# A transformer block on one core: the opening of its first feed-forward layer taken one token tile at a time

## The chip, the cores and the metric

The kernel runs on one core of a Trainium2 chip. The metric is device time in microseconds (us) of one launch, the median of three runs. The core has five engines that run in parallel, each with its own in-order list of instructions: TensorE (PE in the profile; its weight loads are PEld), VectorE (DVE), ScalarE (ACT), GpSimd (POOL) and SyncE (SP), which here only issues transfers. SBUF is the on-chip memory; PSUM holds what PE accumulates.

## The reference, cut to what matters

One block: a feed-forward layer (FFN), a mixer of attention and convolution, a second FFN. Each is preceded by an RMS norm whose result is modulated by a shift and a scale, and followed by a gate. Shifts, scales and gates are 9 x 2048 numbers, one product of a vector with a matrix of 2048 x 18432 (151 MB). There are 256 tokens, D = 2048, F = 5632, all in fp32.

```
ada = einsum('bd,de->be', silu(c), w_ada) + b_ada
sh1, sc1, g1, shm, scm, gm, sh2, sc2, g2 = split(ada, 9)
h = modulate(rms_norm(x, ffn1_norm), sh1, sc1)      # h * (1 + sc) + sh
x = x + 0.5 * g1 * swiglu(h, ffn1_w_gu, ffn1_w_down)
```

## The kernel before

**Tiles.** The 256 tokens are two token tiles of 128 (t = 0, 1). The depth of 2048 is 16 slices of 128, which this document calls k-rows; four of them are one piece (kb or pc, 0 to 3). The 2 x 5632 columns of the first product are 22 chunks of 512 columns (256 of the gate, 256 of the other half). A "row" of work is one k-row of one chunk for both token tiles. Every operand is split into a high and a low part, and a product is three matmuls (`mm3`, lines 315 to 317): high x high, high x weight's low, low x weight's high. A row is thus six matmuls of 128x512. A weight comes as fp32 from memory; ACT casts its high part (lines 294, 308), DVE subtracts to get the low part (lines 296, 309).

**The ada lines.** `w_ada` is stored as 144 lines of 1 MB, each 128 outputs x 2048. `ada(j)` (line 175) loads line j into one of four buffers (`rawp`, shared with the 1 MB weight tiles) and reduces it on DVE against `c_bc`, the activated c spread over all partitions. A k-row of the normed input needs two lines, its scale and its shift; for the first FFN, k-row k needs lines 2k and 2k+1. `ada_due` (line 195) spreads the loads: `DUE` is a table of (rows of work, lines to have asked for by then), read by straight lines between its points.

**The opening of the first FFN** (`ffn`, line 441, branch `if not st.done`, lines 479 to 516). The order is written out:
- At line 116 to 118 the small constants and both token tiles of x are loaded. Lines 746 to 748 sum the squares of both tiles. `begin_both` (line 390) normalizes the first 512 columns of both tiles and transposes them into two PSUM buffers.
- `first_modulation` (line 228) loads lines 0 and 1 in halves, with chunk 0's first weight row between them, and reduces each half.
- `begin_ready` modulates a k-row for both tiles as soon as its two lines have been asked for: `Norm.tile` (line 380), one ACT and two DVE operations.
- Chunks 0 to 7 first run with one k-row, 8 to 11 with two, 12 to 14 with three, the others with all four of the first piece (`EXT`). `LOADS` says which chunks share a transfer; work on a load follows its transfer by `AHEAD` = 3 loads. `FIRST_ADA` gives the ada lines asked for after each of the first twelve loads; after that `DUE` does. The result of a chunk goes from PSUM to a part in SBUF by an ACT copy (line 468).

**After the opening.** The chunks of `AGAIN` (4, 5, 6) get the rest of their first piece in PSUM, which `add_part` (line 535, DVE) adds to the part. `EARLY` lists groups of chunks that then run their rest with pieces 1 and 2. The second normed piece is made when ada lines up to 16 have been asked for (`pieces`). All else comes later and is not touched.

**What sets the order.** The program's text gives the order in which work is offered; a list scheduler places an instruction on its engine as soon as its estimated time comes, so that a later one that is ready can go ahead of an earlier one that is not. `tc.issue_after(ins)` keeps what it encloses behind `ins` on the same engine's list. Buffers come from pools: 28 blocks of 4 KB a partition (`blkp`), four each of high and low weight buffers of two rows (`whp`, `wlp`), six PSUM accumulators, two PSUM buffers for transposes.

## Time and profile before

| | |
|---|---|
| Median of 3 runs | 1859.41 us (1859.16 to 1860.31) |
| The profiled execution | 1858.73 us |
| Its span | 1857.0 us, granted TensorE clock 0.994 |
| PE busy | 1823.5 us, 98% |
| DVE busy | 1442.8 us, 78% |
| ACT busy | 910.7 us, 49% |
| Transfers | 495.91 MB, 267 GB/s on average |

The span runs from the first to the last instruction of the program; the execution's own time is 1.7 us longer. "Busy" counts an engine's own instructions, not waits. A row of the timeline is: start, duration, engine and line, operation, what it writes and from what, and in brackets how long the engine had been idle and what ended that. A row of the waits is: who waited for whom, total us, times, longest. "PEclk" is the clock granted to TensorE, 1.00 being full. SPq is SP issuing a transfer; the transfer's data comes later.

### The profile page before, as it was taken

Reading aid. Unit: us, or ns where it says so; the run is one execution under the profiler, and the core shown is the slowest. Engines: PE = TensorE matmul, PEld = TensorE weight load, DVE = VectorE, ACT = ScalarE, POOL = GpSimd, SP = SyncE. Lnnn points to the kernel's source line nnn. Section 1 sums busy time; section 2 is a strip of 40 time slices with the busy share of each in tenths; the row PEclk is TensorE's granted clock in tenths of the full one; section 3 lists DMA queues with packets and bytes.
Section 4 is the critical chain, followed back from the end, with each engine's and each line's share of the span. In section 5 each row is a group of like instructions: output and inputs, shape, how many; then the busy total and the mean of one; then the engine's idle time right before and its main releaser. Section 6 shows DMA issues by size and latency. Waiting matters only on the chain.

```text
span 1857.0 us, 21888 instructions
## 1 busy us (share of the span) xinstructions
PE 1823.5 (98%) x8247; PEld 1503.3 (81%) x8247; DVE 1442.8 (78%) x1922; ACT 910.7 (49%) x1378; POOL 28.8 (2%) x29
## 2 busy tenths in 40 slices
PE   6999999999999999999999899999999999999999
PEld 5788888888888887888888688888888888888887
DVE  7788869998888778789899968878877755544553
ACT  6553444444444443554776545664444444433332
POOL 0000000000000000000110000000000000000000
PEclk8999999999999999999999899999999999999999
DMA  9888968889989898645444667888777755556552
GB/s 384 336 318 302 344 253 317 336 297 342 328 327 367 341 355 331 241 178 181 159 159 159 249 227 276 338 321 333 269 279 281 281 182 194 191 206 213 196 212 79
DMA packets 72730, 495.91 MB, mean 267 GB/s; under 512 B 8193, under 2 KB 8625, under 8 KB 15153
## 3 DMA queue, kind: packets, MB, share of 16 engines
q1 hardware_dynamic: 72624, 494.53, 71.6%
q8 instruction: 64, 1.05, 0.2%
q14 instruction: 42, 0.34, 0.0%
HBM read 492.37 MB, written 2.12 MB: 266 GB/s over the span
## 4 chain that ended last, share of the span: by engine, by line
PE 91%; DVE 4%; DMA 2%; ACT 1%; issue 1%; POOL 0%; SPq 0%; POOLq 0%; DVEq 0%; ACTq 0%
PE acc L316 30%; PE acc L317 30%; PE acc L315 29%; DMA blk<-in_w_gu_dram 1%; DVE wlo L296 1%; DVE blk L771 1%; PE tp L588 1%; DMA raw<-in_w_ada_dram 1%; PE acc L863 1%; PE tp L377 1%; ACT whi L294 0%; DVE raw L181 0%; ACT tmp L825 0%; POOL rv L978 0%; DVE blk L923 0%
## 5 line engine op out<-in xcount | busy, mean ns | idle before, releaser
L294 ACT CAST whi<-raw 128x1024 fp32r<-128x1024 f32 (+1 forms) x605 | 628.0, 1046 | 751.7 <-PE acc L317 605.8
L296 DVE TENSOR_TENSOR wlo<-raw,whi 128x1024 fp32r<-128x1024 f32 (+1 forms) x605 | 724.7, 1211 | 319.8 <-ACT whi L294 318.7
L315 PE MATMUL acc<-whi,blk 128*128 128x512 f32 x2448 | 957.4, 393 | 10.8 <-ACT blk L990 4.8
L316 PE MATMUL acc<-wlo,blk 128*128 128x512 f32 x2448 | 956.9, 391 | 2.5 <-DVE wlo L296 2.5
L317 PE MATMUL acc<-whi,blk 128*128 128x512 f32 x2448 | 956.1, 391 | 1.1 <-DVE blk L991 1.1
L315 PEld LDWEIGHTS acc<-whi,blk 128*128 128x128 f32 x2448 | 460.9, 188 | 107.3 <-ACT blk L990 5.1
L316 PEld LDWEIGHTS acc<-wlo,blk 128*128 128x128 f32 x2448 | 461.3, 188 | 99.3 <-DVE wlo L296 5.6
L317 PEld LDWEIGHTS acc<-whi,blk 128*128 128x128 f32 x2448 | 460.5, 188 | 98.8 <-DVE blk L991 1.8
L181 DVE CUSTOM_DVE_ANT_0 raw<-raw,c_bc 128x2048 f32<-128x2048 f32 x142 | 324.2, 2284 | 10.1 <-DMA raw<-in_w_ada_dram 9.9
L771 DVE SCALAR_TENSOR_TENSOR blk<-blk,cst,blk 128x255 f32<-128x255 f32 (+14 forms) x240 | 97.6, 458 | 0.0
L468 ACT COPY blk<-acc 128x512 f32<-128x512 f32 x88 | 49.8, 591 | 60.3 <-PE acc L317 58.4
L580 DVE TENSOR_TENSOR blk<-acc,blk 128x512 f32<-128x512 f32 x88 | 56.7, 682 | 0.1
L315 PE MATMUL acc<-blk,blk 128*128 128x512 f32 x112 | 43.9, 393 | 0.0
L317 PE MATMUL acc<-blk,blk 128*128 128x512 f32 x112 | 43.8, 391 | 0.0
L316 PE MATMUL acc<-blk,blk 128*128 128x512 f32 x112 | 43.6, 389 | 0.0
L296 DVE TENSOR_TENSOR blk<-raw,blk 128x1024 fp32r<-128x1024 f32 x28 | 33.8, 1220 | 2.1 <-ACT blk L294 1.9
L582 DVE TENSOR_TENSOR blk<-blk 128x256 f32<-128x256 f32 x88 | 33.3, 417 | 0.5 <-ACT blk L581 0.5
L581 ACT ACTIVATE blk<-blk 128x256 f32<-128x256 f32 x88 | 32.2, 411 | 1.4 <-DVE blk L580 1.4
L294 ACT CAST blk<-raw 128x1024 fp32r<-128x1024 f32 x28 | 28.9, 1050 | 7.7 <-DMA raw<-in_w_dn_dram 6.5
L334 DVE TENSOR_TENSOR blk<-tp,blk 128x512 fp32r<-128x512 f32 x44 | 29.9, 684 | 1.8 <-ACT blk L333 1.8
L343 ACT ACTIVATE tmp<-xall 128x512 f32<-128x512 f32 x22 | 13.8, 632 | 30.1 <-DVE xall L641 16.7
L333 ACT CAST blk<-tp 128x512 fp32r<-128x512 f32 x44 | 25.3, 580 | 2.4 <-PE tp L588 2.4
(149 smaller groups left out, 665.9 us busy)
## 6 DMA issues: line engine op xcount, KB each, us to landing
raw<-in_w_gu_dram SPq DMA_DIRECT2D x161, 1024.0 KB, 5.3
raw<-in_w_ada_dram SPq DMA_DIRECT2D x142, 1024.0 KB, 6.2
raw<-in_w_dn_dram SPq DMA_DIRECT2D x88, 1024.0 KB, 4.9
raw<-in_w_in_dram SPq DMA_DIRECT2D x40, 1024.0 KB, 4.8
raw<-in_w_out_dram SPq DMA_DIRECT2D x16, 1024.0 KB, 4.7
raw<-in_w_gu_dram SPq DMA_DIRECT2D x8, 768.0 KB, 5.5
blk<-in_w_gu_dram SPq DMA_DIRECT2D x10, 512.0 KB, 13.9
blk<-gate_line SPq DMA_DIRECT2D x6, 512.0 KB, 6.9
```

What stands on the lines that cost most here:

```text
L181: nc.vector.tensor_tensor_reduce(out=raw, in0=raw, in1=c_bc, scale=1.0, scalar=0.0, op0=ALU.mult, op1=ALU.add, accum_out=ada_cols[g][:, j ...
L294: nc.scalar.copy(out=hi[:, :m, :], in_=rw)
L296: nc.vector.tensor_sub(out=lo[:, :m, :], in0=rw, in1=hi[:, :m, :].bitcast(F32))
L315: nc.tensor.matmul(acc, ah, wh, start=start, stop=False)
L316: nc.tensor.matmul(acc, ah, wl, start=False, stop=False)
L317: return nc.tensor.matmul(acc, al, wh, start=False, stop=stop)
L334: nc.vector.tensor_sub(out=lo, in0=tp, in1=hi.bitcast(F32))
L468: last_part[0] = nc.scalar.copy(out=parts[c][:, t, :], in_=accs[t])
L580: nc.vector.tensor_add(out=p[:, t, :], in0=accs[t], in1=p[:, t, :])
L581: nc.scalar.activation(out=p[:, t, :256], in_=p[:, t, :256], func=AF.Silu)
L582: nc.vector.tensor_mul(out=p[:, t, 256:], in0=p[:, t, :256], in1=p[:, t, 256:])
L771: nc.vector.scalar_tensor_tensor(out=y[:, d:], in0=u, scalar=w, in1=y[:, d:], op0=ALU.mult, op1=ALU.add)
```

## The change

Five things are changed, all in the opening of the first FFN and just behind it.

1. At the start only tile 0 of x is loaded. Tile 1's load follows the weights of the first three loads (`X_BEHIND` = 2). The squares of a tile are now summed in `begin_one(t)`, two of four slices on DVE for both tiles (before: tile 0 only).
2. Nothing stands between the four halves of ada lines 0 and 1.
3. The first five loads (`BY_TILE`, chunks 0 to 7) go with their one k-row through tile 0, then through tile 1. The k-row is modulated for each tile by itself. High and low parts of chunks 4 to 7 lie in blocks, not in the weight buffers.
4. Chunks 0 to 9 have one k-row in the opening, 10 to 14 two, 15 to 17 three, 18 to 21 four (45 rows; before 53). `FIRST_ADA` is gone: `DUE` rules from the start, with new points.
5. `AGAIN` also has 7, 15, 16 and 17.

```diff
-EXT = (1,) * 8 + (2,) * 4 + (3,) * 3
-LOADS = [(0,), (1,), (2, 3), (4, 5), (6, 7)] + [(c,) for c in range(8, NCH)]
-FIRST_ADA = (0, 0, 1, 1, 1, 1, 1, 0, 1, 1, 1, 1)
-AGAIN = [4, 5, 6]
+EXT = (1,) * 10 + (2,) * 5 + (3,) * 3
+LOADS = [(0,), (1,), (2, 3), (4, 5), (6, 7), (8, 9)] + [(c,) for c in range(10, NCH)]
+BY_TILE = 5
+X_BEHIND = 2
+AGAIN = [4, 5, 6, 7, 15, 16, 17]
-DUE = ((19, 8), (55, 16), (107, 24), (150, 32))
+DUE = ((8, 4), (17, 6), (26, 8), (57, 16), (107, 24), (150, 32))
...
-    for t in range(NT):
-        nc.sync.dma_start(out=xall[:, t, :], in_=x_in[t * P:(t + 1) * P, :])
+    def load_x(t):
+        return nc.sync.dma_start(out=xall[:, t, :], in_=x_in[t * P:(t + 1) * P, :])
+
+    load_x(0)
...
-        r0, j0 = 0, 2
-        for r, j in DUE:
+        r0, j0 = DUE[0]
+        for r, j in DUE[1:]:
...
-    def first_modulation(between):
+    def first_modulation():
...
-                between(2 * i + h)
...
-        hi = whp.tile([P, 2, 512], F32R, tag="whi", name=nm("whi"))
-        lo = wlp.tile([P, 2, 512], F32R, tag="wlo", name=nm("wlo"))
+        hi = blk([P, 2, 512], F32R) if held else whp.tile([P, 2, 512], F32R, tag="whi", name=nm("whi"))
+        lo = blk([P, 2, 512], F32R) if held else wlp.tile([P, 2, 512], F32R, tag="wlo", name=nm("wlo"))
...
+        def begin_one(self, t):
+
+            self.done.add((0, t))
+            for n in range(4):
+                square_sum(n, t, self.ss, n % 2 == 1)
+            self.rstd(t)
+            xn = tmp([P, 512])
+            nc.scalar.activation(out=xn, in_=x[0][:, t, :], func=AF.Identity, scale=self.r[t])
+            for j in range(4):
+                nc.tensor.transpose(self.raws[j][:, t * P:(t + 1) * P], xn[:, j * P:(j + 1) * P], ident)
...
-            first_modulation(lambda n: load(0) if n == 3 else None)
+            st.begin_first()
+            st.begin_one(0)
+            first_modulation()
+            begun[0] = 1
+            for t in range(NT):
+                ts = slice(t * P, (t + 1) * P)
+                st.tile(st.raws[0][:, ts], tmp([P, P]), (0, ts))
+                for i in range(BY_TILE):
+                    if t == 0:
+                        load(i)
+                        if i == X_BEHIND:
+                            with tc.issue_after(w_dma[0].ins):
+                                w_dma[0] = load_x(1)
+                            st.begin_one(1)
+                        rows[0] += len(LOADS[i])
+                    for c in LOADS[i]:
+                        stage_a(c, ws[c], {t: acc_tile()}, (t,), 1)
+                if t == 0:
+                    with tc.issue_after(w_dma[0].ins):
+                        ada_due(rows[0])
             begin_ready()
-            for i in range(len(LOADS) + AHEAD):
+            for i in range(BY_TILE, len(LOADS) + AHEAD):
...
-                        if i < len(FIRST_ADA):
-                            ada_until(ada_next[0] + FIRST_ADA[i])
-                            rows[0] += ext[LOADS[i][0]] * len(LOADS[i])
-                        else:
-                            ada_a_share(ext[LOADS[i][0]])
+                        ada_a_share(ext[LOADS[i][0]] * len(LOADS[i]))
...
-    for t in range(NT):
-        for n in range(4):
-            square_sum(n, t, norm1.ss, t == 0 and n % 2 == 1)
```

More of the change, by code (lines that the diff above doesn't have):

```diff
@@ L299, in w_tile, with w_first @@
         return lambda j: views[j]
-    def w_first(cs):
+    def w_first(cs, held):
         n = len(cs)
@@ L479, in ffn @@
         if not st.done:
-            raws, begun = st.begin_both(), [0]
+            begun = [0]
             ws = {}
@@ L486, in load, with begin_ready @@
                 if ext[cs[0]] == 1:
-                    ws.update(zip(cs, w_first(cs)))
+                    ws.update(zip(cs, w_first(cs, X_BEHIND < i < BY_TILE)))
                 else:
                     ws[cs[0]] = w_tile(w_gu[cs[0], 0], False, (0, ext[cs[0]]), ext[cs[0]] < 4)
+            def begin_ready():
+                while begun[0] < 4 and base + 2 * begun[0] + 2 <= ada_next[0]:
+                    st.tile(st.raws[begun[0]], tmp([P, S]), (begun[0], slice(0, S)))
+                    begun[0] += 1
@@ L491, in ffn @@
             for c in range(NCH):
                 ext[c] = EXT[c] if c < len(EXT) else 4
-            def begin_ready():
-                while begun[0] < 4 and base + 2 * begun[0] + 2 <= ada_next[0]:
-                    st.tile(raws[begun[0]], tmp([P, S]), (begun[0], slice(0, S)))
-                    begun[0] += 1
-            first_modulation(lambda n: load(0) if n == 3 else None)
+            st.begin_first()
+            st.begin_one(0)
+            first_modulation()
+            begun[0] = 1
@@ new lines, in ffn @@
+            first_cs = [c for cs in LOADS[:BY_TILE] for c in cs]
+            for t in range(NT):
[14 more added lines that the diff above has]
+                        ada_due(rows[0])
@@ L499, in ffn @@
             begin_ready()
[L500 removed]
+            for i in range(BY_TILE, len(LOADS) + AHEAD):
                 if i < len(LOADS):
[L502 to L503 removed]
+                    load(i)
                     with tc.issue_after(w_dma[0].ins):
[L505 to L509 removed]
+                        ada_a_share(ext[LOADS[i][0]] * len(LOADS[i]))
@@ L745, in block_kernel @@
     norm2 = Norm(96, "n2", sm([P, NT, 4], "ss"))
-    for t in range(NT):
-        for n in range(4):
-            square_sum(n, t, norm1.ss, t == 0 and n % 2 == 1)
     ffn(norm1, w_gu1, w_dn1, 32, (0.78, 32), (0.78, 104), norm_m, AGAIN, EARLY, EARLY_3)
```

14 lines of the change are left out of this document (3 added, 11 removed).

## The prediction

> **What bounds the kernel now.** First the page's head, then a table of busy time by stretches up to 123 us (columns: stretch, its length, then busy us and instructions of PE, PEld, DVE, ACT, POOL, then granted clock, DMA share, GB/s).
>
> ```profile
> span 1857.0 us, 21888 instructions
> ```
> ```profile
> 0.00:17.66 17.66, 5.90 (x24) 4.71 (x24) 8.03 (x22) 9.76 (x23) 2.32 (x7) 0.82 0.90 335
> 17.66:20.00 2.34, 2.33 (x5) 1.61 (x6) 2.31 (x4) 1.87 (x3) 0.00 (x0) 0.50 1.02 409
> 20.00:57.00 37.00, 34.09 (x140) 25.90 (x140) 36.03 (x44) 25.94 (x43) 0.00 (x0) 0.98 1.02 415
> 57.00:66.00 9.00, 6.85 (x22) 4.86 (x21) 5.16 (x6) 5.33 (x7) 0.00 (x0) 0.81 0.86 341
> 66.00:90.00 24.00, 24.00 (x107) 19.88 (x106) 16.89 (x18) 12.54 (x17) 0.00 (x0) 1.00 0.80 298
> 90.00:123.00 33.00, 33.00 (x151) 27.39 (x151) 27.78 (x41) 18.71 (x30) 0.00 (x0) 1.00 0.75 276
> ```
> From 66 us on PE is busy without a break: there PE is the bound, and the change adds and removes no matmul. What it can move is what PE loses before that. Until 57 us two others are full: DVE (36.03 of 37.00) and the transfers (share 1.02, 415 GB/s).
>
> I count PE's work in rows: one 128-deep slice of one chunk for both token tiles, six matmuls. The copies of finished accumulators (line 468) give the pace.
>
> ```profile
> 84.13 0.59 ACT L468 COPY blk<-acc 128x512 f32<-128x512 f32 x1 [0.98 <-PE acc L317]
> ...
> 89.57 0.59 ACT L468 COPY blk<-acc 128x512 f32<-128x512 f32 x1 [3.23 <-PE acc L317]
> ```
> Four rows in 89.57 - 84.13 = 5.44 us: 1.36 us a row, 0.227 a matmul. Line 468 has 39 copies up to there, two a chunk, so the last one opens chunk 19. Chunks 0 to 19 are 8x1 + 4x2 + 3x3 + 5x4 = 45 rows, and chunk 19's last three matmuls follow: row 45 ends at 89.57 + 0.68 = 90.25.
>
> ```profile
> 17.67 0.80 PE L315 MATMUL acc<-whi,blk 128*128 128x512 f32 x1 [2.17 <-ACT blk L386]
> ```
> ```profile
> PE acc L315 <- ACT blk L386: 2.2, 1, 2.2
> PE acc L315 <- ACT whi L294: 2.0, 2, 1.6
> PE acc L315 <- ACT blk L468: 1.8, 2, 1.1
> PE acc L316 <- DVE wlo L296: 1.3, 3, 0.5
> ```
> The first row starts at 17.67. Without loss row 45 would end at 17.67 + 45 x 1.36 = 78.87; it ends 11.4 later. Of that 5.1 are waits (2.0 + 1.8 + 1.3; the 2.2 lies before 17.67) and 3.6 half clock: 0.50 x 2.34 + 0.02 x 37 + 0.19 x 9. The rest is slow restarts.
>
> **The change, term by term.**
>
> *Start.* From 8.63 on SP issues only as older transfers land, so these starts are landings: the second x, three halves of the first two ada lines, chunk 0's row, the last half.
>
> ```profile
> 8.63 0.34 SPq L180 DMA_DIRECT2D raw<-in_w_ada_dram  x1
> 10.53 0.38 SPq L305 DMA_DIRECT2D blk<-in_w_gu_dram  x1
> 11.80 0.33 SPq L180 DMA_DIRECT2D raw<-in_w_ada_dram  x1
> 13.11 0.38 SPq L305 DMA_DIRECT2D blk<-in_w_gu_dram  x1
> 13.77 0.33 SPq L180 DMA_DIRECT2D raw<-in_w_ada_dram  x1
> 15.07 0.33 SPq L289 DMA_DIRECT2D blk<-in_w_gu_dram  x1
> ```
> ```profile
> 6.14 0.69 DVE L340 CUSTOM_DVE_ANT_0 tmp<-xall 128x512 f32<-128x512 f32 x1 [2.85 <-DMA xall<-in_x_dram]
> ...
> 8.18 0.15 DVE L141 TENSOR_SCALAR rstd<-rstd 128x1 f32<-128x1 f32 x1
> ...
> 13.20 0.22 DVE L241 SCALAR_TENSOR_TENSOR ada<-adah,cst 128x1 f32<-128x1 f32 x1
> 13.46 0.16 DVE L245 SCALAR_TENSOR_TENSOR scales<-ada,cst 128x1 f32<-128x1 f32 x1
> 13.53 1.22 DVE L239 CUSTOM_DVE_ANT_0 blk<-blk,c_bc 128x1024 f32<-128x1024 f32 x1
> 13.60 0.72 ACT L398 ACTIVATE tmp<-xall,rstd 128x512 f32<-128x512 f32 x1 [1.63 <-POOL rstd L142]
> ...
> 15.47 1.22 DVE L239 CUSTOM_DVE_ANT_0 blk<-blk,c_bc 128x1024 f32<-128x1024 f32 x1
> ```
> The first x lands at 6.14 as now; the gain is in what follows it. The second x (8.63 - 6.14 = 2.49) and chunk 0's row (13.77 - 13.11 = 0.66) leave the queue ahead of the last half, which then lands at 15.07 - 3.15 = 11.92. DVE is later: free at 8.33, three reductions (3.66) and the two small operations (0.33) bring the fourth to 12.4. From the fourth's start to the first matmul took 17.67 - 15.47 = 2.20; so 14.6, or **-3.1**. Bounds: -3.6 (landing, 11.92 + 2.20 = 14.1) and -0.5 (chunks 0 to 3's lows, 2.6, put between the reductions).
>
> *One-row part.* By the intervals above and 1.27 per 512 KB (10.53 to 11.80), landings are: chunks 0 to 3 by 14.6, x of tile 1 at 17.1, chunks 4 to 7 by 19.7, ada 2 and 3 at 22.2 and 24.7, chunks 8 and 9 at 26. The x of tile 1 is a new wait. Behind its squares on ACT stand the casts of chunks 4 to 7, behind its transposes on PE whatever the list puts there, behind its transfer on SP all later ones. DVE's low halves take 0.68 for one row and 1.22 for two (rows of lines 537, of that size, and 296 below). From 14.2 on it makes row 0 of tile 0 (0.8) and chunks 0 to 3 (2.6) to 17.6, two squares and the mean (1.7) to 19.3, chunks 4 to 7 (landed at 19.7, cast in about 1) to 22.0. So PE ends the tile-0 half near 22.7. Tile 1 is ready after pow (1.63 was ACT's wait for it), scaling (0.72), transposes and modulation (estimated at two us together): near 23.6. Its 24 matmuls (5.4) end at 29.0; 48 matmuls alone would end at 14.6 + 10.9 = 25.5, so 3.5 are lost. DVE's two ada lines and chunk 8's low follow from 24 on (2 x 2.45 + 1.22, to 30.1): about 0.9 more, as chunk 8's first matmul needs no low. From row 10 to 45 both suppliers fit: DVE 35 x 0.61 + 8 ada x 2.45 + two modulations of 1.0 = 43.0, transfers (35 x 0.262 + 8 x 1.05 MB) / 415 GB/s = 42.3, PE 47.6. Before, ada 8 to 10 ran ahead of their use in this stretch; now they come after row 29. Own loss 4.4 in place of 11.4: **-7.0**. Bounds: -9.4 (own loss of one half-clock stretch alone, 2.0) and -2.6 (rival 1's 4.4 on top). Chunks 4 to 7's halves in block buffers cost nothing while 23 of 28 are taken (8 parts, 2 of row 0, 4 ada halves, 5 raw, 4 held); else a load waits 1.22 for a low.
>
> ```profile
> 62.82 0.63 PE L315 MATMUL acc<-whi,blk 128*128 128x512 f32 x1
> 63.25 0.63 PE L316 MATMUL acc<-wlo,blk 128*128 128x512 f32 x1
> ```
> At 0.43 a matmul PE runs here at half pace, right after waits of 1.6 and 0.5. The Trainium skill (TensorE: Matmul & The Clock Gate, Part 1) says that the clock halves only after an idle window of about 3.4 us and returns after a busy one. By that rule the opening pays for one cold window and the sum stays as it is; by this trace, where waits that short did cost pace, a second one is possible and the sum is 1.7 higher.
>
> *Rows 29 to 60, now the tight place.* Four chunks more are finished by an extra addition each; the ada table asks for lines 8 to 16 within 31 rows. DVE's groups up to 123 us (behind the bar: busy us, mean ns, then idle before):
>
> ```profile
> L181 DVE CUSTOM_DVE_ANT_0 raw<-raw,c_bc 128x2048 f32<-128x2048 f32 x16 | 36.6, 2285 | 0.4 <-DMA raw<-in_w_ada_dram 0.3
> L296 DVE TENSOR_TENSOR wlo<-raw,whi 128x1024 fp32r<-128x1024 f32 x20 | 23.9, 1221 | 13.8 <-ACT whi L294 13.8
> ...
> L537 DVE TENSOR_TENSOR blk<-acc,blk 128x512 f32<-128x512 f32 x6 | 3.8, 679 | 0.0
> ...
> L425 DVE TENSOR_SCALAR tmp<-tp,scales,ada 128x128 f32<-128x128 f32 x4 | 1.4, 400 | 0.0
> ```
> DVE: 31 x 0.61 = 18.9, nine ada lines at 2.285 and a small operation of 0.16 like line 245's: 22.0, fourteen additions 9.5, the second norm piece 4 x 0.40 + 2 x 0.68 = 3.0: 53.4 us, against 42.2 of PE; transfers (17.6 MB) need 42.3. Row 29 falls at 14.6 + 39.4 + 4.4 = 58.4. DVE can lead by some 6 us (four low buffers of two rows, 4.9, and half an ada line); the last two chunks' additions and one line (4 x 0.68 + 2.45 = 5.1) may come after row 60. Then 48.3 us run from 52.4 and end at 100.7, while PE would end row 60 at 100.6: no stall, the lower bound. Without that deferral, and at the share of 90 to 123 us (27.78 / 33.00 = 0.84), they end at 52.4 + 63.6 = 116.0, the upper: +15.4. With deferral at 0.84: 109.9; without, at 0.974 (36.03 / 37.00): 107.2; with it at 0.974: 102.0. I take 105.5, between these last three, since ready work is put ahead in part: **+4.9**. It is a wait of PE for low halves, and accumulators held by additions.
>
> *After row 60*: chunks 12 to 14 have a row more left, 15 to 17 and 7 less; the total of rows is the same, and at PE's full pace it hides DVE at 0.84. Extra casts and split modulations (under 1 us of DVE) are in the 6 us of lead; uncovered they cost that 1 us.
>
> Sum: -3.1 - 7.0 + 4.9 = -5.2.
>
> **The rivals.**
> 1. *The tile-1 half stands in the way.* Its transposes come ahead of chunks 4 to 7 in PE's order, so 12 matmuls (2.7) wait behind x, and a second half-clock stretch like that of 57 to 66 us costs 0.19 x 9 = 1.7. For it: waits of 1.6 and 0.5 already cost pace. Against: in the list ready work goes first. -5.2 + 4.4 = -0.8: 1858.7.
> 2. *No stall up to row 60.* DVE at 97% (as in 20 to 57) with deferral: -10.1, 1849.4. Against it: transfers too would need all of their time.
> 3. *DVE becomes the bound, slower.* In rows 29 to 60 the additions wait for PE in DVE's order and nothing is deferred: row 60 at 116.0 against 90.25 + 15 x 1.36 = 110.65 before: +5.4, 1864.8. It decides below a DVE share of 53.4 / (110.65 - 52.4) = 0.92. For it: 0.70 and 0.84 after 66 us; against: PE was the bound then, and DVE's 13.8 us of waits were for casts that waited for PE.
>
> **How the numbers follow.** The profiled execution took 1858.73 us (span 1857.0 and 1.7 around it), 0.68 under the median 1859.41: 1858.73 - 5.2 = 1853.5, as a median 1854.2. Chances: forecast 0.48 (its own range 1851 to 1858), rival 1 0.20, rival 2 0.14, rival 3 0.18. A measurement tells 0.2%, 3.7 us, from no change: below 1855.7 is faster, above 1863.1 slower. Faster: 0.38 of the forecast, 0.06 of rival 1, all of rival 2: 0.58. Same: 0.10 and 0.14: 0.24. Slower: rival 3, 0.18. The range reaches from just under rival 2 to most of rival 3: 1848.6 to 1864.
>
> **What would show it.** Start: the first matmul of line 315's kind at 14.1 to 15.5, not after 17. One-row part: the tile-1 half beginning near 23.6 and no wait over 1.6 before it; the granted clock back at 1.0 by 25. Row 45 near 80, read from the copies of chunk 21. Stall: PE waiting for lows near 95 to 106, DVE above 0.9 there. The forecast is wrong if PE is idle for 4 us between 15 and 30, or if DVE has idle time while PE waits for its lows.

## The result, and the profile after

The changed kernel takes 1875.98 us (1875.23 to 1877.10, six runs) against 1859.29 us of the kernel before in the same runs: a ratio of 1.0086, with a 95% interval of 1.0073 to 1.0099. It is slower by 16.7 us. The forecast was 1854.2, and the range ended at 1864.

The table of busy time by stretches of the kernel after (same columns as in the prediction):

```profile
20.00:30.00 10.00, 5.95 (x14) 2.96 (x13) 4.69 (x10) 5.94 (x11) 0.55 (x1) 1.00 1.02 400
30.00:40.00 10.00, 8.34 (x21) 5.68 (x22) 5.97 (x7) 4.56 (x8) 0.00 (x0) 1.00 1.02 410
...
90.00:123.00 33.00, 27.24 (x124) 21.10 (x122) 28.68 (x44) 13.99 (x23) 0.00 (x0) 1.00 0.74 267
123.00:160.00 37.00, 35.48 (x144) 28.37 (x145) 34.51 (x46) 16.27 (x18) 0.00 (x0) 0.91 0.93 354
```

There are two places where PE is not busy: up to 40 us, and from 90 to 160 us. In the first DVE is not busy either (4.69 of 10, 5.97 of 10). PE's timeline there, only the matmuls with an idle time before them:

```profile
15.01 0.79 PE L318 MATMUL acc<-whi,blk 128*128 128x512 f32 x1 [1.78 <-ACT whi L311]
18.29 0.79 PE L318 MATMUL acc<-whi,blk 128*128 128x512 f32 x1 [1.19 <-ACT whi L311]
21.86 1.22 PE L318 MATMUL acc<-whi,blk 128*128 128x512 f32 x2 [1.62 <-ACT whi L311]
26.49 1.12 PE L408 MATMUL tp<-cst,tmp 128*128 128x128 f32 x4 [1.30 <-ACT tmp L406]
28.66 1.22 PE L318 MATMUL acc<-blk,blk 128*128 128x512 f32 x2 [1.05 <-ACT blk L311]
33.61 1.22 PE L318 MATMUL acc<-blk,blk 128*128 128x512 f32 x2 [1.62 <-ACT blk L311]
```

PE waits for ACT each time. So the next view is ACT's timeline in the same stretch:

```profile
17.14 0.58 ACT L475 COPY blk<-acc 128x512 f32<-128x512 f32 x1 [2.18 <-PE acc L320]
17.62 0.62 ACT L311 CAST whi<-blk 128x512 fp32r<-128x512 f32 x1
20.27 0.59 ACT L475 COPY blk<-acc 128x512 f32<-128x512 f32 x1 [2.04 <-PE acc L320]
20.76 1.05 ACT L311 CAST whi<-blk 128x1024 fp32r<-128x1024 f32 x1
...
27.57 1.03 ACT L311 CAST blk<-blk 128x1024 fp32r<-128x1024 f32 x1
31.18 0.59 ACT L475 COPY blk<-acc 128x512 f32<-128x512 f32 x1 [2.57 <-PE acc L320]
32.03 0.58 ACT L475 COPY blk<-acc 128x512 f32<-128x512 f32 x1 [0.27 <-PE acc L320]
32.51 1.05 ACT L311 CAST blk<-blk 128x1024 fp32r<-128x1024 f32 x1
```

The casts (line 311) of 17.62, 20.76 and 32.51 stand behind copies (line 475) for which ACT waited two microseconds or more for PE; that of 27.57 stands behind two more copies and tile 1's scaling and modulation. ACT is idle while the next load's weights lie there (e7 below casts chunks 2 and 3 at 15.73, as they land), because the copy of the chunk before is ahead in its list. So each load is a full circle: cast, low half on DVE, matmuls, copy, and only then the next cast. The Trainium skill (TensorE: Matmul & The Clock Gate, Architectural detail) says that ACT and DVE are strict first-in-first-out; these rows agree.

The second place, PE's timeline behind row 45 (the copies of chunk 21 are at 94.06 and 94.74, so row 45 ends at 94.74):

```profile
100.70 0.50 PE L319 MATMUL acc<-wlo,blk 128*128 128x512 f32 x1 [0.58 <-DVE wlo L299]
106.61 0.50 PE L319 MATMUL acc<-wlo,blk 128*128 128x512 f32 x1 [1.53 <-DVE wlo L299]
112.44 0.50 PE L319 MATMUL acc<-wlo,blk 128*128 128x512 f32 x1 [1.46 <-DVE wlo L299]
123.00 0.50 PE L319 MATMUL acc<-wlo,blk 128*128 128x512 f32 x1 [2.19 <-DVE wlo L299]
125.11 1.22 PE L318 MATMUL acc<-whi,blk 128*128 128x512 f32 x2 [0.86 <-ACT whi L297]
126.99 1.22 PE L318 MATMUL acc<-whi,blk 128*128 128x512 f32 x2 [0.66 <-ACT whi L297]
```

Here the balance of the two kernels:

| | before | after |
|---|---|---|
| first matmul | 17.67 | 15.01 |
| row 45 ends | 90.25 | 94.74 |
| lost in between, beyond 45 x 1.36 | 11.4 | 18.5 |
| PE's waits from row 45 to 160 us | none | 7.3 |
| clock lost from 123 to 160 us (0.09 x 37) | none | 3.3 |
| span | 1857.0 | 1873.7 |

The start gives 2.66, the one-row part takes 7.1, and what follows row 45 takes 12.2 (16.7 - 4.5); the waits and the clock are 10.6 of that. By the count of the matmuls row 60 ends at 124.2 (before: 111.4), so 8.3 are lost up to there and 3.9 behind it. From 160 us on the two traces run parallel, 16 to 17 us apart.

### The profile page after: what moved, and what is told of

Same layout as the page of the kernel before. It is cut to its first block, busy times and chain, and to the rows that moved or that the text cites. A ratio compares the mean times of both kernels' runs of the same rounds, so it can differ in the third digit from the quotient of the medians.

```text
span 1873.7 us, 21911 instructions
## 1 busy us (share of the span) xinstructions
PE 1832.1 (98%) x8247; PEld 1506.7 (80%) x8247; DVE 1449.4 (77%) x1937; ACT 911.1 (49%) x1376; POOL 28.8 (2%) x29
## 3 DMA queue, kind: packets, MB, share of 16 engines
q8 instruction: 64, 1.05, 0.2%
## 4 chain that ended last, share of the span: by engine, by line
PE 91%; DVE 5%; ACT 1%; issue 1%; DMA 1%; POOL 0%; SPq 0%; POOLq 0%; DVEq 0%; ACTq 0%
PE acc L319 30%; PE acc L320 29%; PE acc L318 29%; DVE wlo L299 1%; DVE blk L791 1%; PE tp L611 1%; PE acc L883 1%; PE tp L380 0%; DMA raw<-in_w_gu_dram 0%; DVE raw L185 0%; DMA blk<-in_w_ada_dram 0%; DMA raw<-in_w_ada_dram 0%; ACT whi L297 0%; DVE blk L242 0%; DVE blk L560 0%
## 5 line engine op out<-in xcount | busy, mean ns | idle before, releaser
L603 DVE TENSOR_TENSOR blk<-acc,blk 128x512 f32<-128x512 f32 x88 | 56.7, 683 | 0.1
L318 PE MATMUL acc<-blk,blk 128*128 128x512 f32 x120 | 47.9, 404 | 2.7 <-ACT blk L311 2.7
L319 PE MATMUL acc<-blk,blk 128*128 128x512 f32 x120 | 48.1, 401 | 0.1
L320 PE MATMUL acc<-blk,blk 128*128 128x512 f32 x120 | 47.9, 400 | 0.0
L560 DVE TENSOR_TENSOR blk<-acc,blk 128x512 f32<-128x512 f32 x44 | 29.0, 686 | 5.8 <-PE acc L320 5.7
L318 PEld LDWEIGHTS acc<-blk,blk 128*128 128x128 f32 x120 | 22.8, 192 | 8.1 <-ACT blk L311 3.8
```

The source lines that it names most:

```text
L318: nc.tensor.matmul(acc, ah, wh, start=start, stop=False)
L319: nc.tensor.matmul(acc, ah, wl, start=False, stop=False)
L320: return nc.tensor.matmul(acc, al, wh, start=False, stop=stop)
L603: nc.vector.tensor_add(out=p[:, t, :], in0=accs[t], in1=p[:, t, :])
```

## The experiments

Two theories came first. **A, the order of the lists:** casts behind copies on ACT in the opening, low halves behind additions on DVE later. **B, the suppliers:** DVE's time and the transfers set both losses, in whatever order. In the table, "row 45" and "waits" (sum of PE's idle times over 0.1 us from row 45 to 160 us) are of the profiled execution (for e6, e9 and e18, whose chunk 21 ends with row 48, row 45 is that end less 3 x 1.36); the ratio is against the kernel before on the same chip.

| | time, us | ratio (95%) | row 45 | waits |
|---|---|---|---|---|
| after | 1875.98 | 1.0086 (1.0073 to 1.0099) | 94.7 | 7.3 |
| e1 casts first | 1873.18 | 1.0078 (1.0063 to 1.0093) | 91.8 | 8.2 |
| e2 old lengths | 1869.65 | 1.0063 (1.0046 to 1.0080) | 94.2 | 3.8 |
| e3 old opening | 1864.85 | 1.0034 (1.0022 to 1.0045) | 84.7 | 7.6 |
| e4 other order behind row 45 | 1876.50 | 1.0095 (1.0079 to 1.0110) | 94.4 | 6.0 |
| e5 = e3, ada lines sooner | 1867.19 | 1.0042 (1.0027 to 1.0057) | 86.6 | 6.1 |
| e6 = e3, fewer additions | 1860.76 | 1.0008 (0.9998 to 1.0017) | 84.9 | 4.7 |
| e7 = e1, tile 1 first | 1864.49 | 1.0028 (1.0016 to 1.0040) | 82.7 | 7.0 |
| e8 idle matmuls at the start | 1874.42 | 1.0079 (1.0063 to 1.0096) | 94.7 | 8.0 |
| e9 = e7 with e6 | 1859.63 | 1.0004 (0.9995 to 1.0014) | 84.1 | 4.7 |
| e10 = e7, additions spread | 1862.79 | 1.0014 (1.0005 to 1.0024) | 83.3 | 5.9 |
| e11 = e7, old lengths | 1859.41 | 1.0000 (0.9991 to 1.0010) | 84.8 | 3.7 |
| e12 = e3, additions spread | 1863.46 | 1.0023 (1.0014 to 1.0032) | 83.9 | 5.9 |
| e13 = e7, half of DVE's ada work | 1865.49 | 1.0038 (1.0024 to 1.0052) | 83.2 | 7.8 |
| e14 = e13, half of the transfers too | 1857.87 | 0.9992 (0.9983 to 1.0002) | 82.3 | 2.1 |
| e15 = e7, no additions | 1864.61 | 1.0030 (1.0018 to 1.0042) | 82.9 | 6.5 |
| e16 = e7, other buffers | 1867.81 | 1.0053 (1.0038 to 1.0068) | 83.2 | 8.9 |
| e17 = e14, other half set aside | 1873.23 | 1.0074 (1.0061 to 1.0088) | 93.6 | 5.3 |
| e18 = e9, later ada lines | 1856.35 | 0.9986 (0.9977 to 0.9995) | 84.4 | 1.9 |

### The opening: e1, e2, e3, e7, e8

**e1** loads and casts chunks 0 to 7 first and keeps tile 0's copies behind the last cast on ACT's list.

```diff
-                for i in range(BY_TILE):
-                    if t == 0:
-                        load(i)
...
+                if t == 0:
+                    for i in range(BY_TILE):
+                        load(i)
...
+                    with tc.issue_after(last_cast[0].ins) if t == 0 else nullcontext():
                         for c in LOADS[i]:
                             stage_a(c, ws[c], {t: acc_tile()}, (t,), 1)
```

> All casts of chunks 0 to 7 are put ahead of the tile-0 copies in ACT's order (the first squares of tile 1 fall behind them too); nothing is left out. Theory A (the order: in the changed kernel a cast whose data has landed stands behind a copy that waits for PE, so each chunk of the tile-0 half is one round trip): the tile-0 half shrinks from 21.7 us (15.0 to 36.7) to 13 to 16, the tile-1 half starts at 29 to 31, and the time falls by 5 to 8 us, to 1868 to 1871. Theory B (suppliers: late transfers, a full DVE and PE at half clock set the pace, the order only shows it): the tile-1 half starts no earlier than 34 and the time stays within 2 us of 1876.

It took 1873.18 us. ACT's timeline of e1, then PE's wait behind tile 0's half:

```profile
19.71 1.05 ACT L313 CAST blk<-blk 128x1024 fp32r<-128x1024 f32 x1 [2.78 <-DMA blk<-in_w_gu_dram]
23.29 1.04 ACT L313 CAST blk<-blk 128x1024 fp32r<-128x1024 f32 x1 [2.53 <-DMA blk<-in_w_gu_dram]
...
31.31 0.72 ACT L408 ACTIVATE tmp<-xall,rstd 128x512 f32<-128x512 f32 x1 [1.87 <-POOL rstd L146]
```
```profile
32.09 1.11 PE L410 MATMUL tp<-cst,tmp 128*128 128x128 f32 x4 [4.66 <-ACT tmp L408]
```

The casts now wait for the transfers alone: chunks 4 and 5 are cast at 19.71 where the kernel after casts them at 27.57, chunks 6 and 7 at 23.29 in place of 32.51. Tile 0's half ends at 27.43 instead of near 36.7. But tile 1's squares stood behind those casts and behind copies (the second at 25.80), an ada line of 2.28 us on DVE ahead of the row factor, and POOL's power took 2.53 us; PE stood idle 4.66 us for the transposes. Row 45 came only 2.9 us sooner, and the time alone can't be told from the kernel after's (the intervals of the ratios overlap). The casts did what A said; its time was missed because a second thing was late.

**e7** puts tile 1's squares, scaling and modulation ahead of tile 0's copies as well.

```diff
                         if i == X_BEHIND:
                             with tc.issue_after(w_dma[0].ins):
                                 w_dma[0] = load_x(1)
-                            st.begin_one(1)
+                            with tc.issue_after(last_cast[0].ins):
+                                st.begin_one(1)
                         rows[0] += len(LOADS[i])
```

> e1 (casts of chunks 0 to 7 ahead of the copies on ACT, 1873.18 us) with the squares, the row factor and the transposes of token tile 1 issued right behind the casts and ahead of the copies, so that they don't stand behind tile 0's copies. In e1 the PE stood idle 4.66 us for them. Theory A (ACT's list order sets the opening): the idle stretch between the halves falls under 1.5 us, row 45 ends at 87 to 89 in place of 91.8, and what comes behind row 45 takes back no more than 1 us: 1868 to 1871. Theory B (DVE and the transfers set row 45, whatever the order): row 45 stays at 91 or later and the time at 1872 to 1875.

It took 1864.49 us, 3.5 us below the lower of A's bounds, with row 45 at 82.7. ACT's timeline and PE's waits of e7:

```profile
18.21 0.63 ACT L348 ACTIVATE tmp<-xall 128x512 f32<-128x512 f32 x1 [1.44 <-DMA xall<-in_x_dram]
...
19.80 1.05 ACT L313 CAST blk<-blk 128x1024 fp32r<-128x1024 f32 x1 [0.26 <-DMA blk<-in_w_gu_dram]
...
22.37 1.04 ACT L313 CAST blk<-blk 128x1024 fp32r<-128x1024 f32 x1
23.30 6.63 ACT L477 COPY blk<-acc 128x512 f32<-128x512 f32 x13
```
```profile
20.90 0.73 PE L320 MATMUL acc<-blk,blk 128*128 128x512 f32 x2 [0.77 <-ACT blk L313]
23.94 0.99 PE L320 MATMUL acc<-blk,blk 128*128 128x512 f32 x2 [0.58 <-ACT blk L477]
31.61 1.20 PE L320 MATMUL acc<-whi,blk 128*128 128x512 f32 x4 [0.26 <-ACT whi L313]
```

The instructions are those of the kernel after; what was changed is the order in which ACT takes them, and through it when the others can start. PE waits 1.6 us between the first matmul and 31.61 where the kernel after waits 6.8 (1.19 + 1.62 + 1.30 + 1.05 + 1.62) up to 33.61. Row 45 moves by 12.0 us, the time by 11.5 (10.8 by the two ratios). Of the 12.0, 5.2 are these waits; most of the rest is pace, since matmuls stood 0.43 apart up to 38.45 in the kernel after and up to 18.7 here. The order of ACT's list is shown to be what the change lost in the opening.

**e8** puts matmuls that nobody reads ahead of the first real one, in order to have the clock up.

```diff
+    warm_up(22)
...
             st.begin_one(0)
+            with tc.issue_after(last_tp[0].ins):
+                warm_up(12)
```

> The kernel after with matmuls added on PE that nobody reads: 22 of 256 columns at the very start and 12 behind tile 0's transposes, so that the PE is busy up to the first real matmul. They leave everything else as it is. If the half pace of the first 23 us (0.43 us for a matmul of 512 columns up to 38.45) is a cause of its own, the tile-0 half gets shorter and row 45 ends 3 to 6 us sooner: 1870 to 1873. If the round trips over ACT's list set the half, the pace within them is worth little: row 45 within 1.5 us of 94.7 and 1874.5 to 1876.5.

Row 45 at 94.65, time 1874.42: the first matmuls do run faster (the first copy comes at 16.65, not 17.14), but the circles over ACT stay. This does not test the pace within them: the matmul at 18.53 takes 0.78 again, and from 23.21 on they stand 0.42 apart. In e7 the pace came back with the order alone.

**e3** is the kernel before with the new lengths and tables alone, **e2** the kernel after with the old lengths.

```diff
-EXT = (1,) * 8 + (2,) * 4 + (3,) * 3
+EXT = (1,) * 10 + (2,) * 5 + (3,) * 3
-LOADS = [(0,), (1,), (2, 3), (4, 5), (6, 7)] + [(c,) for c in range(8, NCH)]
+LOADS = [(0,), (1,), (2, 3), (4, 5), (6, 7), (8, 9)] + [(c,) for c in range(10, NCH)]
-AGAIN = [4, 5, 6]
+AGAIN = [4, 5, 6, 7, 15, 16, 17]
-DUE = ((19, 8), (55, 16), (107, 24), (150, 32))
+DUE = ((8, 4), (17, 6), (26, 8), (57, 16), (107, 24), (150, 32))
```

> The kernel of before with the new lengths, loads, additions and ada table alone; both tiles of x at the start and both tiles together. Theory A: no loss by tile, row 45 ends at 85 to 90, the waits for low halves behind it stay (7 to 11 us): 1862 to 1870. Theory B: the longer one-row part takes load off DVE and the transfers, so it is faster than before, 1850 to 1856.

> The opening by token tile is kept; the lengths go back (8 chunks of one row, 4 of two, 3 of three, loads and the chunks finished by additions as before); the ada table stays the new one. Theory A (two separate losses, one of the by-tile order, one of the additions and ada lines in DVE's order behind row 45): the second goes, the first stays: 9 to 12 us less than the changed kernel, 1864 to 1867, still slower than before by 5 to 8. Theory B (suppliers): the ada lines are only needed earlier, so the waits move into the opening and the time stays above 1872.

e3: row 45 at 84.7, 5.5 us sooner than before with the same first matmul (17.92). So the new lengths and tables work in the opening. But the waits behind row 45 are nearly those of the kernel after (0.58, 1.53, 1.46, 2.18, then 1.86 in three), and the time is 1864.85.

e2 keeps the slow opening (row 45 at 94.2) with waits of 3.8: 1869.65, above the 1864 to 1867 that A asked for and below the 1872 of B. Each loss stands without the other: the opening by tile loses in ACT's order, the lengths and tables lose behind row 45.

### Behind row 45: the order, the additions, the ada lines

**e4** puts the next chunk's low half ahead of the additions and the ada line on DVE's list.

```diff
             w = w_tile(w_gu[g, 0], False, (ext[g], 4))
+            after_low(last_low[0])
...
-            add_part(g, accs)
-            ada_a_share(3)
-            pieces(last_part[0])
+            owed.append((g, accs))
```

> The changed kernel, with each addition and ada line of the chunks 4, 5, 6, 7, 15, 16, 17 put behind the next chunk's low half in DVE's order; nothing else. Theory A: PE's waits for low halves from 100 to 127 us (7.3 us, and 3 us of half clock behind them) fall to under 3, the time by 6 to 9 us, to 1867 to 1870. Theory B (DVE has too much work there in any order): the waits move but their sum stays above 6, and the time within 2 us of 1876.

1876.50, no gain in time, as B expected. But the trace shows that the order counts here too. In the kernel after, low halves stand in DVE's list behind two additions (line 560), which must wait until PE has ended the chunk before:

```profile
98.14 1.37 DVE L560 TENSOR_TENSOR blk<-acc,blk 128x512 f32<-128x512 f32 x2 [3.24 <-PE acc L320]
99.43 1.82 DVE L299 TENSOR_TENSOR wlo<-raw,whi 128x1024 fp32r<-128x1024 f32 x2
```

In e4 PE has no wait before 112.61: the three waits at 100 to 112 us are gone, and row 57 ends at 111.76 (in the kernel after: 116.20). All of it is lost again behind that, in three waits for casts (3.1 us), one for transposes (1.4) and half pace. ACT had to wait for the weights to land before two of these casts:

```profile
114.78 0.62 ACT L298 CAST whi<-raw 128x512 fp32r<-128x512 f32 x1 [2.09 <-DMA raw<-in_w_gu_dram]
...
121.86 1.56 ACT L298 CAST whi<-raw 128x1024 fp32r<-128x1024 f32 x2 [2.00 <-DMA raw<-in_w_gu_dram]
```

So behind row 45 A is right about the first waits, and something else, close behind it, holds the time.

**e5** and **e6** tell apart the ada lines that the new table puts there (theory D) and the additional additions (theory C), both from e3.

```diff
-DUE = ((8, 4), (17, 6), (26, 8), (57, 16), (107, 24), (150, 32))
+DUE = ((8, 4), (17, 6), (26, 8), (45, 14), (57, 16), (107, 24), (150, 32))
```
```diff
-EXT = (1,) * 10 + (2,) * 5 + (3,) * 3
+EXT = (1,) * 10 + (2,) * 5
-AGAIN = [4, 5, 6, 7, 15, 16, 17]
+AGAIN = [4, 5, 6]
```

> The kernel before with the longer one-row part alone (e3, 1864.85 us) with one more point in the table of due lines, (45, 14): about two ada lines (2.28 us of DVE each, 4.6 us together) move from behind row 45 into the one-row part, where the shares of rows 36 to 57 left DVE some time. Theory D (the ada lines that the new table puts off are what stalls the PE behind row 45): the waits behind row 45, 7.4 us in e3, fall by about 4 us and row 45 stays near 85: 1859 to 1861. Theory C (the four additional chunks of one row and their additions are the cause, the ada lines only pass the wait on): 1863 to 1866, the waits behind row 45 the same within 1.5 us.

> e3 (1864.85 us) with chunks 15 to 17 taken whole and chunks 4 to 6 alone multiplied again, as before the change, so ten chunks of one row and five of two remain. Between 57 and 123 us e3 has 14 additions of 0.69 us on DVE where the kernel before has 6: four chunks, eight additions, 5.5 us of DVE less here, and four loads for a part of a piece less. Theory C (the additional additions and part loads are the cause of the stall behind row 45): the waits behind row 45 fall from 7.4 us to under 3 and the half-pace stretch at 125 goes: 1855 to 1859. Theory D (the ada lines put off by the table): 1863 to 1866.

e5 took 1867.19 (by the ratios 1.0042 against e3's 1.0034, not told apart): the lines moved forward made a new wait of 1.62 us up to 69.10, ahead of row 45. D as it was put, with 1859 to 1861, falls. e6 took 1860.76, with waits of 4.7: C's direction, but short of its 1855 to 1859.

**e15** leaves out the additions behind the chunks multiplied again altogether; **e10** and **e12** only move them.

```diff
-            add_part(g, accs)
             ada_a_share(3)
```
```diff
-AGAIN = [4, 5, 6, 7, 15, 16, 17]
+AGAIN = [4, 5, 6]
...
                 start_of[c] = upto
+            if ext[15] < 4 or ext[16] < 4 or ext[17] < 4:
+                again_one(15 + i_g)
```

> e7 with the additions behind the chunks multiplied again left out (14 of 0.69 us; these chunks' sums lack the product of their last rows of the first piece). The additions, by their time or by the wait for PE that stands in DVE's list ahead of the next low half, are the cause: the waits behind row 45 fall under 1.5 us and the half pace goes, 10 us in all: 1853 to 1856. DVE's total time is the cause: 9.6 us of DVE are gone, the same saving is possible, but the waits of 0.57 and 1.53 us, which come behind only two additions, stay. Buffers and transfers are the cause: waits of over 4 us stay: 1859 to 1863.

> e7 (1864.49 us) with the multiplying again kept to chunks 4 to 6: chunk 7's rows go to the group of the EARLY table that holds it, and chunks 15, 16 and 17 (one row each left, with two additions each) behind the first three groups of EARLY, one behind each. The opening, its lengths and the number of additions stay; only the place of eight additions moves. If the place counts (short chunks one behind another, 1.36 us of PE against 2.0 us of DVE): three of the six waits behind row 45 (2.18 + 0.63 + 0.66 us) and the half pace at 115 to 121 (3.3 us) go: 1858 to 1861. If the number of additions counts (5.5 us more of DVE before 160 us): new waits in the rows of EARLY of the same size, 1863 to 1866.

> e3 (the kernel before with the new lengths, 1864.85 us) with chunks 7, 15, 16 and 17 placed as in e10. The opening is that of the kernel before. Place counts: waits behind row 45 fall from 7.4 us to about 4 and the half pace goes, 1857.5 to 1860.5. Number counts: 1863 to 1866.

e15 took 1864.61, the time of e7: 9.6 us of DVE are gone, and nothing is won. DVE now stands 4.36 us for PE's transposes, ahead of a low half, and at 110.63 PE waits 3.60 us for a cast for which ACT had waited 5.15 us, until the weights landed. The additions alone are not what sets the time. Spreading them gives 1.7 and 1.4 us; e10 lies between its two expectations, e12 in that of the number, and the intervals of their ratios overlap those of e7 and e3.

**e13** and **e14** take the ada lines apart: half of DVE's work on lines 8 to 23, then half of their transfer as well.

```diff
+        n_c = 1024 if 8 <= j < 24 else D
-        nc.vector.tensor_tensor_reduce(out=raw, in0=raw, in1=c_bc, scale=1.0, scalar=0.0, op0=ALU.mult,
+        nc.vector.tensor_tensor_reduce(out=raw[:, :n_c], in0=raw[:, :n_c], in1=c_bc[:, :n_c], scale=1.0, scalar=0.0, op0=ALU.mult,
```
```diff
+        n_d = 1024 if 8 <= j < 24 else D
-        nc.sync.dma_start(out=raw, in_=w_ada[j])
+        nc.sync.dma_start(out=raw[:, :n_d], in_=w_ada[j][:, :n_d])
```

> e7 (1864.49 us, 7.0 us of waits behind row 45 and half pace behind them) with DVE reducing only the first 1024 columns of ada lines 8 to 23 (their sums leave out the other half); the transfers stay whole. DVE's time is the cause: 16 lines shorter by about 1.1 us, half of them before 123 us, so the waits fall under 3 us: 1855 to 1859. Buffers and transfers, or the additions' wait for PE, are the cause: the waits stay within 2 us: 1861.5 to 1865.

> As e13, and the transfer of these lines is halved too (0.5 MB in place of 1 MB). DVE's time is the cause: as e13 within 1.5 us. Transfers and the raw buffers are the cause: the weights land sooner and the raw buffers come free sooner, another 3 us or more below e13. The additions' wait for PE is the cause: 1861 to 1865, as e13.

With half of DVE's work the time is as in e7 (1865.49). In the kernel after DVE is full while PE waits for it, busy 31.15 of the 32.02 us from 98.14 on (e7: 31.31 of 31.87 from 86.13 on). In e13 it is busy 28.25 of 31.50 from 86.50 on, and yet the waits are 7.8 us (e7: 7.0); those for low halves fall from 5.7 to 5.1, those for casts rise from 1.3 to 2.7. Ahead of the waits DVE is far from full. The stretch of e13 from 57 to 90 us (DVE 21.69 of 33; before 88 us PE has no wait there):

```profile
57.00:90.00 33.00, 32.43 (x148) 26.69 (x147) 21.69 (x32) 19.07 (x27) 0.00 (x0) 1.00 0.84 322
```

With half of the transfers as well it is 1857.87, 7.6 us less on the same chip. The transfers of e13 and then of e14 from 57 to 110 us (issues, KB each, median us from issue to landing), and PE's waits in e14:

```profile
raw<-in_w_ada_dram SPq DMA_DIRECT2D x8, 1024.0 KB, 7.3
raw<-in_w_gu_dram SPq DMA_DIRECT2D x6, 768.0 KB, 5.6
```
```profile
raw<-in_w_gu_dram SPq DMA_DIRECT2D x7, 768.0 KB, 5.8
raw<-in_w_ada_dram SPq DMA_DIRECT2D x8, 512.0 KB, 6.0
```
```profile
104.58 0.73 PE L322 MATMUL acc<-whi,blk 128*128 128x512 f32 x2 [0.59 <-ACT whi L301]
106.56 0.89 PE L322 MATMUL acc<-whi,blk 128*128 128x512 f32 x2 [1.25 <-ACT whi L301]
107.71 1.11 PE L384 MATMUL tp<-cst,tmp 128*128 128x128 f32 x4 [0.25 <-ACT tmp L378]
```

A load of weights does not land faster in e14 (5.8 against 5.6); it is asked for sooner, and one more falls into the stretch. But the transfers are not all that differs. Where e13's DVE waits 4.30 us for PE with two additions ahead of the next low halves (86.56 to 89.6), e14's has a low half (86.63) between one addition and the next. No run changes the transfers and keeps the lists as they are.

So DVE is the one PE names, and it is full; but to take work from it (e13, e15) or to mend its list (e4) wins nothing while the transfers stay whole. What lies close behind is the supply through SP. The waits of SP's queue in e7 from 57 to 115 us:

```profile
SPq L288 <- DVE wlo L301: 16.1, 6, 6.1
SPq L288 <- DVE tmp L434: 9.5, 2, 6.3
SPq L184 <- DVE ada L185: 8.8, 5, 2.1
```

The columns are us in total, times, the longest. Line 288 loads weights and line 184 ada lines, both into the four raw buffers. These three rows alone are 34 of 58 us in which SP stood until DVE was done with something, in the first and the third with the last reading of a raw buffer; the buffer then takes some 7 us to fill (medians of 6.6 to 7.0 in e7 from 768 KB up). So DVE and the transfers wait for each other in turn.

**e16** loads the weights of the chunks multiplied again into blocks, **e17** is e14 with the second half of each line moved into DRAM, so that the bytes are there again without holding a buffer.

```diff
-            w = w_tile(w_gu[g, 0], False, (ext[g], 4))
+            w = w_tile(w_gu[g, 0], False, (ext[g], 4), True)
```
```diff
+        if n_d < D:
+            aside = dramp.tile([P, 1024], F32, name=nm("aside"))
+            nc.sync.dma_start(out=aside, in_=w_ada[j][:, n_d:])
```

> e7 with the weights of the chunks multiplied again loaded into buffers of the other pool in parts of two rows, so that they don't wait for one of the four raw buffers that the ada lines share. The raw buffers are the cause: the casts come sooner, the waits behind row 45 fall by 3 us or more: 1858 to 1861.5. DVE's time or the additions are the cause: the low halves are as late as before: 1863 to 1866, more if the other pool has no buffer free.

> e14 (1857.87 us) with the other half of each of the ada lines 8 to 23 moved too, into DRAM, by a transfer of its own behind the first: the bytes read are again those of e13, but none of these second halves holds a raw buffer, and nobody waits for it (the lines' sums leave it out, as in e13 and e14). Bytes are the cause: the weights behind land as late as in e13 and the waits behind row 45 come back: 1862 to 1867. Buffers are the cause: 1857 to 1860.

Neither settles it. In e16 (1867.81) PE loses 4.4 us at 83 to 90 us, where e7 loses 0.57. The trace shows the order of the lists once more: chunk 4's cast began at 84.91, but its low half stands in DVE's list behind modulations, for which DVE waited 4.09 us for PE, and behind an ada line of 2.28 us, and starts at 88.32. In e17 (1873.23) the transfers that nobody waits for were put at the front of SP's queue: three went ahead of the first weights, the first matmul came at 17.91 instead of 14.93 and row 45 at 93.6. It tests another thing than was meant; its waits behind row 45 are 5.3 us, against 2.1 in e14. Whether the bytes, the time in the buffer or the order of the lists counts most stays open.

### Two repairs together, and a lower demand: e9, e11, e18

**e9** is e7 with e6's lengths, **e11** e7 with the old lengths, and **e18** is e9 with one number of the table changed.

```diff
-DUE = ((8, 4), (17, 6), (26, 8), (57, 16), (107, 24), (150, 32))
+DUE = ((8, 4), (17, 6), (26, 8), (63, 16), (107, 24), (150, 32))
```

> The two halves of the change mended at once: e7's order of ACT's list in the opening by tile (row 45 at 82.7) and e6's lengths behind it (ten chunks of one row, five of two, chunks 4 to 6 alone multiplied again). If the opening by tile and the additions behind it are two separate causes, their gains add: e6 against e3 gave 4.1 us, e3 with e7's opening would start from 1864.5: 1858.5 to 1861.5. If what the opening saves is always paid back behind row 45, because DVE has so much work for these rows by 160 us whatever the opening (it is busy 34 to 36 of 37 us from 123 to 160 in every kernel), it comes out as e6 did, 1860 to 1862, with waits behind row 45 longer than e6's 4.7 us by what row 45 is sooner.

> e7's opening by tile with the lengths of the kernel before (eight chunks of one row, four of two, three of three, chunks 4 to 6 again), the new table of due lines. It answers whether the opening by tile, with its list mended, is worth anything alone: e2 (the same lengths, list not mended) took 1869.65 us with row 45 at 94.2. If the list was all that was wrong there, row 45 comes at 83 to 86 and the waits behind it stay at e2's 4.3 us: 1857 to 1861. If the lengths of before can't feed a sooner opening (rows of the fourth load still to land), row 45 comes at 87 or later: 1861 to 1865.

> e9 (1859.63 us; row 45 early, few additions) with the point (57, 16) of the table of due lines moved to (63, 16): 8 lines over 37 rows in place of 31, so 0.216 MB of ada lines a row in place of 0.258, beside 0.25 MB of weights in 1.36 us. If the bytes asked for per row between rows 26 and 60 set the waits behind row 45, they fall from 4.7 us to 2 to 3.5: 1856.5 to 1858.5, which would be below the kernel before by about 0.1%. If the second block of the activation, which needs line 16, becomes late instead, the PE waits longer for its transposes: 1860 to 1864.

e9 and e11 are level with the kernel before, 1.0004 and 1.0000. e18 takes 1856.35 against 1859.07, ratio 0.9986 (0.9977 to 0.9995): 2.7 us below the kernel before, and 3.3 below e9. Its waits from 85 to 130 us are these two:

```profile
98.97 0.50 PE L321 MATMUL acc<-wlo,blk 128*128 128x512 f32 x1 [0.92 <-DVE wlo L301]
128.71 0.50 PE L321 MATMUL acc<-wlo,blk 128*128 128x512 f32 x1 [1.01 <-DVE wlo L301]
```

It suggests a measure that parts the kernels in two: what the table asks of the transfers in a row. A row's weights are 0.262 MB, an ada line 1.05 MB, a row takes 1.36 us. Before, 8 lines over rows 19 to 55: 0.262 + 0.233 MB, 364 GB/s. New table, 8 over 31 rows: 0.262 + 0.271, 392 GB/s. e5, 6 over 19: 436. e14, half lines: 292. e18, 8 over 37: 359. The best that any stretch of the prediction's table shows is 415. The kernels at 364 and below (before, e14, e18) have waits of 0 to 2.1 us behind row 45; those at 392 and above have 3.7 and more. It is no measured limit: at 392, e6 moved 373 GB/s from 57 to 90 us, and e9 and e18 moved 338 and 336 from 57 to 110 us. And e18's list differs from e9's as e14's does from e13's: e9's DVE waits 3.24 us with two additions ahead of a low half (91.58), e18's makes that low half first (91.28). Low halves stand ahead in the kernel before too; e2 and e11, with its lengths and the new table, have additions ahead at their waits. Since e15 wins nothing, e6's gain is not in its additions alone; what else it has less of behind row 45 is four loads through the four buffers. All this is argued, not isolated by a run. At 0.14% the gain of e18 is also smaller than the 0.2% that the prediction took as the least one can tell; its interval, from eleven runs, lies below 1.

## Why the prediction was wrong

**Start: right.** Forecast 14.6 for the first matmul, measured 15.01; -3.1 against -2.66, within its bounds.

**One-row part: the step that failed first.** Forecast -7.0, measured +7.1. The walk let ACT cast each load about 1 us after it landed ("landed at 19.7, cast in about 1") and DVE follow; PE was to end tile 0's half near 22.7. The landing was right (e1 casts these chunks at 19.71), the cast was not: at 27.57, behind copies that wait for PE. The prediction reckoned with casts behind tile 1's squares, and relied on "in the list ready work goes first". ACT's list put the copies of each chunk ahead of the next cast; why the scheduler's estimates did that no run shows. That ACT held two kinds of work, one ahead of PE and one behind it, was not walked through. e7, where the order is as the prediction had assumed, has the own loss 82.7 - 15.1 - 61.2 = 6.4: the term then is -5.0, against -7.0 forecast, within its bounds of -9.4 and -2.6.

**Rival 1** named part of it: tile 1's transposes did come ahead of chunks 4 to 7, and half pace came too, up to 38.45. But its price, 4.4, was made of one wait and one stretch; there were five waits (6.8 us) and half pace between them.

**Rows 29 to 60: sign right, size short, and half of the mechanism missing.** Forecast +4.9; measured 8.3 between row 45 and row 60, within the bound of 15.4. The term was worked out from DVE's sum (53.4 us against 42.2 of PE), and DVE was full there, but not for that reason alone: the term counted on "ready work is put ahead", and the list put additions that wait for PE ahead of low halves. Nor does DVE alone set the time: halving its part in the ada lines changed nothing (e13), nor did taking away the additions (e15) or mending the list (e4). The text had the other number at hand: transfers need 42.3 us in 42.2 of PE, that is all of the time. It was used only against rival 2. Which of the two weighs more stays open; the time moved where both the transfers and the lists were other (e14, e18).

**After row 60: wrong.** The lead was to absorb the rest. The wait of 2.19 us (at 123.00) is for the low half of chunk 17, row 60; those of 0.86 and 0.66 us are for casts of the first loads behind it, for which ACT waited 3.81 us until they landed. Half pace followed, 3.3 us from 124 to 131. For these 3.9 us behind row 60 the sum had no term.

**Rival 3** had the sign and the place of the second loss. Its mechanism, additions that wait for PE in DVE's order, is in the trace, but e4 and e15 take it away and win no time. That its 1864.8 is nearly e3's and e7's time is luck: e3's row 45 comes 5.5 us and e7's 7.5 us sooner than the 90.25 it reckoned from. The range missed since it held no case in which both terms turn: +7.1 and +12.2 with -2.7 are what was measured.

**The signs set out beforehand** did show it in part. "PE idle for 4 us between 15 and 30": 1.19 + 1.62 + 1.30 + 1.05 = 5.2. The tile-1 half began at 36.7, not near 23.6; row 45 ended at 94.7, not near 80. The sign "DVE has idle time while PE waits for its lows" did not show: DVE was busy in each of these waits. It stood idle for 3.24 us just ahead of the first, which no sign named.

## What to carry to other kernels

When an engine makes inputs for PE and also empties PE's results, walk its list in order and not only its sum: a cast behind a copy turns every load into a full circle, and here the order alone was worth 11.5 us. When PE names one engine as late, take work from that engine before believing it; here that moved the waits to the next limit, the landing of weights, and won nothing. When a list scheduler places the work, compare the lists of two kernels before putting their difference down to the one thing that was edited: here shorter transfers also changed what stood ahead of what.

## What the runs showed that was not expected

The granted clock in the profile can miss a slow stretch. In the kernel after it reads 1.00 from 20 to 40 us (its first clock record lies at 38.7, the return to full clock, and nothing is recorded ahead of it), while PE's timeline shows matmuls 0.43 apart up to 38.45 and 0.23 apart from then on:

```profile
38.02 0.63 PE L318 MATMUL acc<-whi,blk 128*128 128x512 f32 x1
38.45 0.49 PE L319 MATMUL acc<-wlo,blk 128*128 128x512 f32 x1
...
39.01 0.39 PE L318 MATMUL acc<-whi,blk 128*128 128x512 f32 x1
39.24 0.40 PE L319 MATMUL acc<-wlo,blk 128*128 128x512 f32 x1
```

In e2, with the same opening, the same stretch (33 to 38 us) reads 0.52. The Trainium skill (TensorE: Matmul & The Clock Gate, Seeing it yourself) warns that the clock's trace events have been seen to be unreliable; this case agrees, and the distance of the matmuls is the safer reading. The Trainium skill (TensorE: Matmul & The Clock Gate, Part 1) asks for an idle window of about 3.4 us before the clock drops. The measured waits are shorter: in the kernel after, the granted clock drops at 124.0, behind a wait of 2.19 us (at 123.00), and in the kernel before, matmuls stand 0.43 apart at 62.82, behind waits of 1.62 and 0.53.

The power on POOL for one number a partition took 2.53 us in e1 (at 28.74, line 146). In the kernel after the same operation took 0.55 (POOL's one instruction from 20 to 30 us in the table of stretches). What makes the difference was not tried.
